# A fourth buffer for DMA-made weight sums, their loads asked for six steps ahead, and bias rows built in another ring

## The chip, the cores and the metric

The kernel runs on one core of one Trainium2 chip. The metric is the device time of one execution in microseconds (us), the median of several. One execution was profiled as well; all rows come from it.

## The reference, cut to what matters

One layer of an encoder over 512 tokens of width 1024, all in float32:

```python
x = x + 0.5 * swiglu(rmsnorm(x, ffn1_norm), w1, w3, w2)       # feed-forward "a", width 2816
h = rmsnorm(x, mix_norm)
x = x + hybrid_mixer(h, ...)      # h @ w_in, dilated attention (3 groups, T5 bias), grouped-query attention, gates, w_out
x = x + 0.5 * swiglu(rmsnorm(x, ffn2_norm), w1, w3, w2)       # feed-forward "b"
return rmsnorm(x, final_norm)

def swiglu(x, w1, w3, w2):
    return (silu(x @ w1) * (x @ w3)) @ w2
```

The dilated attention adds a bias `bias_tab[t5_bucket(rel)]` to its scores and masks keys outside a window.

## The kernel before, in words

**Three products for one.** A float32 matrix product is made of three products on TensorE: each operand is split into a rounded half H (cast on ScalarE, L211 for weights) and a remainder L (subtraction on VectorE, L212), and `mm3` (L226 to L228) adds H*H, H*L and L*H in PSUM.

**Weights.** All weights pass as tiles of 128x1024. A raw tile comes by DMA into a ring, L211 and L212 make its halves in the ring `wh`/`wl`, and TensorE uses them. Rings (`BUFS`, L19) have a fixed number of buffers: `wr` for plain tiles, and in three stages `wa`, `wt`, `ws` besides. A buffer is loaded again once the last instruction that reads its old tile is done.

**Strassen steps.** In the feed-forward stages (first products of `w1`, `w3`) and in the query/key part of the mixer (`project_qk`), two feature tiles f, f+1 by two halves of the contraction are multiplied by a scheme with seven products instead of eight. The seven steps of a pair are `A11, S1, S2, A12, S3, S4, A22`; each is 24 matmuls of 256 columns. Steps A11, A12 and A22 use a block of the weight as it is. S1 and S3 use a sum of two blocks, which DMA makes: SP loads one block into a `wt` tile (L192), then POOL issues a second transfer that adds the other block into it (L193). S2 and S4 use sums that VectorE makes in a `ws` tile: S2 = S1 + A11 and S4 = S2 + A12 (L210). So a `wt` tile of S1 is read by L210 as well as by L211 and L212. The pairs are interleaved, so that in the steady state the order is A11, S3 (of the pair before), S1, S4 (before), S2, A22 (before), A12. After each step an eviction (`evict`, L452) moves or adds the PSUM bank into a tile `c1` (128x1024, two buffers in pool `c`) or `c2`; after A22, L440 writes the gated result `gg` and `c1` is free. S3 and A22 use the same bank, so A22 can start only when the eviction of S3 (L466, in the query/key stage L726) is done.

**Groups.** Feed-forward "a" makes features 0 to 3 plainly, then three groups by Strassen steps (4 to 7, 8 to 15, 16 to 21), and after each group the rows of `w2` (`blocks`), eight rows d, each ended by an eviction that adds to `x`. "b" is the same with 0 and 1 plain. The query/key stage has one group of five pairs, with evictions of its own (L711).

**Bias rows.** During the `w2` rows of the first group of "a", `side` calls `bias_rows(g)` after rows d = 0, 1, 2: two small loads (a one-hot table and a mask), one product on TensorE (L594), one combination on VectorE (L595) and a store to DRAM from POOL's queue (L596). The three tiles `onehot`, `vmask` and `v` have one buffer each in a pool of their own.

**Order.** TensorE runs in the order in which the program is written. The instructions of the other engines and the DMA issues of SP, ACT and POOL are ordered by a planner at build time: from its own costs it takes, on each engine, the instruction that is ready by its reckoning, and the one that was written first when several are. On the chip each engine and each queue then goes strictly in that order, so one that waits holds up all behind it. When weights are asked for in the written order is set by `todo` (L117): tiles in the order of use, except that a `wt` tile is moved ahead by `EARLY` steps; `ring` (L148) says whether a buffer can be had.

**Row norms.** The sums of squares of a stage's input are made while it already runs; `stat_r` (L382) takes their row sums on TensorE, POOL computes the power -1/2 (L380), and `stat_R` (L391) spreads it by transposes on TensorE (L395). The evictions of the stage's first products wait for it.

Of the kernel before, what the change touches and what calls it, by code (L numbers as in the profile page):

```python
# [11 lines left out]
F32 = mybir.dt.float32  # L12
F32R = mybir.dt.float32r
AF = mybir.ActivationFunctionType
ALU = mybir.AluOpType
PSUM = bass.MemoryType.PSUM
DRAM = bass.MemoryType.DRAM

BUFS = {"wr": 3, "wa": 3, "ws": 2, "wt": 3, "wh": 3, "whx": 1}  # L19
EARLY = 4  # L20
GROUPS = {"a": (4, 8, 16, 22), "b": (2, 8, 16, 22)}
PAIRS = ((0, 0), (1, 0), (0, 1), (0, 2), (1, 1), (1, 2), (2, 0), (3, 0), (2, 1), (2, 2), (3, 1), (3, 2))
NSQ = 10
# [21 lines left out]
V0, V1, V2 = 383, 255, 255  # L45
# [24 lines left out]
class Layer:  # L70
    def __init__(self, ctx, tc, a):
        self.tc, self.nc, self.a = tc, tc.nc, a
        ctx.enter_context(tc.manual_schedule(engines={mybir.EngineType.PE}))
        pool = lambda n, **k: ctx.enter_context(tc.tile_pool(name=n, **k))
        self.dram = pool("dram", bufs=1, space=DRAM)
        self.cst = pool("cst", bufs=1)
        self.wb = pool("wb", bufs=1)
        self.tmp = pool("tmp", bufs=4)
        self.psm = pool("psm", bufs=4, space=PSUM)
        self.psa = pool("psa", bufs=4, space=PSUM)  # L80
        nc = self.nc
        c = self.cst
        self.x = [c.tile([128, T], F32, name=f"x{d}") for d in range(NK)]
        self.par = c.tile([128, 48], F32, name="par")
        nc.scalar.dma_start(self.par, a["par"])
        self.ident = c.tile([128, 128], F32, name="ident")
        self.ones = c.tile([128, 1], F32, name="ones")
        nc.vector.memset(self.ones, 1.0)
        self.mhalf = c.tile([128, 4], F32, name="mhalf")
        nc.vector.memset(self.mhalf, -0.5)  # L90
        nc.scalar.activation(self.ones, self.ones, AF.Copy)
        self.r = c.tile([128, 8], F32, name="r")
        self.R = c.tile([128, T], F32, name="R")
        nc.gpsimd.memset(self.R, 0.0)
        self.acc = c.tile([128, T], F32, name="acc")
        self.open_h()
        self.gate_d = self.dram.tile([16, 128, T], F32, name="gate_d")
        self.qk_d = self.dram.tile([2 * NSQ, 128, T], F32, name="qk_d")
        self.items = ([("v", 0), ("v", 1), ("sw", 0), ("v", 2)] + [("g", j) for j in range(2)]
                      + [("qk", f) for f in range(NSQ, 12)] + [("g", j) for j in range(2, 9)]  # L100
                      + [("b", g) for g in range(3)] + [("g", j) for j in range(9, 16)])
        span = {"v": ("wav", 4), "qk": ("waq", 2), "g": ("wg", 1), "b": ("wb", 4)}
        self.order = self.ffn_order("a")
        for kind, n in self.items:
            if kind == "sw":
                self.order += [("swq", at) for at in self.slots(range(0, NSQ, 2))]
                continue
            name, m = span[kind]
            self.order += [(name, m * n + i) for i in range(m)]
        self.order += [("wab", i) for i in range(12)] + [("wo", i) for i in range(8)]  # L110
        self.order += self.ffn_order("b")
        self.raws, self.tiles, self.used, self.wx, self.TQ = {}, [], 0, None, None
        self.cap = len(self.order)
        self.rings = {k: [] for k in BUFS}
        self.index = {it[:2]: n for n, it in enumerate(self.order)}
        self.kind = [self.home(it) for it in self.order]
        self.todo = sorted((n for n, t in enumerate(self.kind) if t != "ws"), key=lambda n: n - EARLY * (self.kind[n] == "wt"))  # L117

    @staticmethod
    def slots(fs):  # L120
# [27 lines left out]
    def ring(self, tag, n, done, last):  # L148
        held, bufs = self.rings[tag], BUFS[tag]
        pool = self.wb if tag in ("wr", "wh") else self.wx  # L150
        if pool is None or (len(held) >= bufs and held[-bufs] >= done):
            return None
        held.append(last)
        if tag[:2] != "wh":
            return pool.tile([128, 1024], F32, tag=tag, name=tag, bufs=bufs)
        return tuple(pool.tile([128, 1024], F32R, tag=t, name=t, bufs=bufs) for t in ("wh", "wl"))
# [427 lines left out]
    def bias_rows(self, g):  # L584
        nc = self.nc
        n = (V0, V1, V2)[g]
        o = (0, V0, V0 + V1)[g]
        t = {}
        for k, p in (("onehot", 32), ("vmask", 8), ("v", 8)):
            t[k] = self.bp.tile([p, V0], F32, tag=k, name=k)[:, :n]  # L590
            if k != "v":
                nc.sync.dma_start(t[k], self.a[k][:, o:o + n])
        ps = self.aux("bps")
        nc.tensor.matmul(ps[:8, :n], self.rel[:, 8 * g:8 * g + 8], t["onehot"], start=True, stop=True)  # L594
        nc.vector.scalar_tensor_tensor(t["v"], ps[:8, :n], 8.0, t["vmask"], op0=ALU.mult, op1=ALU.add)  # L595
        nc.gpsimd.dma_start(self.vd[:, o:o + n], t["v"])  # L596

    def bias_spread(self, h):
        src = self.vd[h]
# [620 lines left out]
```

## Time and profile before

| What | Value |
|---|---|
| Median of three runs | 1286.1 us (1284.0 to 1286.13) |
| The profiled execution's own time | 1290.42 us |
| Its span, first to last instruction | 1288.7 us |
| Mean granted TensorE clock | 0.996 of full |
| Bytes moved by DMA | 181.91 MB, mean 141 GB/s |
| wt loads: base (SP, L192) and added block (POOL, L193) | 48 of each, 512 KB |
| S2 sums on VectorE (L210, ws<-wt,wa) | 24 |

A row of the timeline has start, duration, engine, line, operation, output<-inputs, count, and in brackets the time that the engine was idle before it and what ended that. A row of a waits view has the total, the number of times and the longest. DMA issues are shown on their queue (SPq, POOL) by the time of issue, not of landing. "issue" means that the profile shows nothing that was waited for.

### The profile page before, as it was taken

Reading aid. Unit: us, or ns where it says so; the run is one execution under the profiler, and the core shown is the slowest. Engines: PE = TensorE matmul, PEld = TensorE weight load, DVE = VectorE, ACT = ScalarE, POOL = GpSimd, SP = SyncE. Lnnn points to the kernel's source line nnn. Section 1 sums busy time; section 2 is a strip of 40 time slices with the busy share of each in tenths; the row PEclk is TensorE's granted clock in tenths of the full one; section 3 lists DMA queues with packets and bytes.
Section 4 is the critical chain, followed back from the end, with each engine's and each line's share of the span. In section 5 each row is a group of like instructions: output and inputs, shape, how many; then the busy total and the mean of one; then the engine's idle time right before and its main releaser. Section 6 shows DMA issues by size and latency. Waiting matters only on the chain.

```text
span 1288.7 us, 19953 instructions
## 1 busy us (share of the span) xinstructions
PE 1270.0 (99%) x8002; PEld 1124.2 (87%) x8002; DVE 883.7 (69%) x1339; ACT 586.5 (46%) x867; POOL 119.2 (9%) x124
## 2 busy tenths in 40 slices
PE   9999999999999999999999999999999999999997
PEld 6897999899889999877888878888889889988996
DVE  7784688468784685767557898655577857774775
ACT  8551355145453443634334466543475415432553
POOL 1011110010210112100001100000201001000001
PEclk9999999999999999999999999999999999999998
DMA  8775677352474866533232310345537537643422
GB/s 301 193 181 171 174 194 183 98 131 67 131 196 131 198 179 219 175 116 92 83 111 82 115 49 25 127 159 190 179 99 179 164 98 185 171 152 99 99 82 66
DMA packets 85549, 181.91 MB, mean 141 GB/s; under 512 B 12480, under 2 KB 19024, under 8 KB 85456
## 3 DMA queue, kind: packets, MB, share of 16 engines
q1 hardware_dynamic: 67904, 140.74, 33.5%
q0 software_dynamic: 16832, 39.34, 15.2%
q8 instruction: 63, 1.03, 0.3%
q10 hardware_dynamic: 720, 0.55, 0.1%
q14 instruction: 30, 0.25, 0.1%
HBM read 168.98 MB, written 15.29 MB: 143 GB/s over the span
## 4 chain that ended last, share of the span: by engine, by line
PE 89%; DVE 4%; issue 2%; ACT 1%; DMA 1%; POOL 0%; SPq 0%; POOLq 0%; DVEq 0%; ACTq 0%
PE mm L226 23%; PE mm L228 23%; PE mm L227 23%; PE Y L226 3%; PE Y L228 3%; PE Y L227 3%; PE X L226 2%; PE X L228 2%; PE X L227 2%; DVE wl L212 1%; PE S L780 1%; PE mm L831 1%; PE Tb L970 1%; PE T L849 1%; PE Sb L227 0%
## 5 line engine op out<-in xcount | busy, mean ns | idle before, releaser
L211 ACT CAST wh<-wr 128x1024 fp32r<-128x1024 f32 x142 | 148.7, 1049 | 218.7 <-PE mm L227 137.6
L212 DVE TENSOR_TENSOR wl<-wr,wh 128x1024 fp32r<-128x1024 f32 x142 | 173.3, 1221 | 56.4 <-ACT wh L211 56.0
L226 PE MATMUL mm<-hH,wh 128*128 128x256 f32 (+1 forms) x600 | 200.0, 333 | 0.5 <-ACT hH L362 0.4
L228 PE MATMUL mm<-hH,wl 128*128 128x256 f32 (+1 forms) x600 | 196.5, 327 | 1.0 <-DVE wl L212 1.0
L227 PE MATMUL mm<-hL,wh 128*128 128x256 f32 (+1 forms) x600 | 196.0, 327 | 0.3 <-DVE hL L363 0.3
L226 PE MATMUL mm<-gg,wh 128*128 128x512 f32 (+1 forms) x376 | 143.2, 381 | 0.0
L228 PE MATMUL mm<-gg,wl 128*128 128x512 f32 (+1 forms) x376 | 142.6, 379 | 0.0
L227 PE MATMUL mm<-gg,wh 128*128 128x512 f32 (+1 forms) x376 | 142.5, 379 | 0.0
L226 PEld LDWEIGHTS mm<-hH,wh 128*128 128x128 f32 x600 | 112.7, 188 | 14.8 <-issue 3.2
L228 PEld LDWEIGHTS mm<-hH,wl 128*128 128x128 f32 x600 | 112.6, 188 | 12.3 <-DVE wl L212 1.4
L227 PEld LDWEIGHTS mm<-hL,wh 128*128 128x128 f32 x600 | 112.7, 188 | 10.4 <-DVE hL L363 0.9
L211 ACT CAST wh<-wa 128x1024 fp32r<-128x1024 f32 x48 | 50.4, 1050 | 102.5 <-PE mm L227 48.0
L494 DVE TENSOR_TENSOR u<-mm,R 128x512 f32<-128x512 f32 (+1 forms) x52 | 33.8, 649 | 85.2 <-PE mm L228 84.9
L226 PE MATMUL mm<-TH,wh 128*128 128x256 f32 x304 | 85.5, 281 | 2.7 <-DVE c L466 2.7
L228 PE MATMUL mm<-TH,wl 128*128 128x256 f32 x304 | 85.6, 281 | 0.0
L227 PE MATMUL mm<-TL,wh 128*128 128x256 f32 x304 | 85.4, 281 | 0.0
L226 PEld LDWEIGHTS mm<-gg,wh 128*128 128x128 f32 x376 | 71.0, 189 | 15.3 <-issue 1.1
L228 PEld LDWEIGHTS mm<-gg,wl 128*128 128x128 f32 x376 | 70.8, 188 | 14.2
L227 PEld LDWEIGHTS mm<-gg,wh 128*128 128x128 f32 x376 | 70.9, 189 | 13.8
L211 ACT CAST wh<-ws 128x1024 fp32r<-128x1024 f32 x48 | 50.4, 1051 | 69.3 <-PE mm L227 51.7
L212 DVE TENSOR_TENSOR wl<-wt,wh 128x1024 fp32r<-128x1024 f32 x48 | 58.6, 1222 | 34.0 <-ACT wh L211 33.6
L211 ACT CAST wh<-wt 128x1024 fp32r<-128x1024 f32 x48 | 50.3, 1050 | 65.0 <-PE mm L227 37.1
(233 smaller groups left out, 3181.5 us busy)
## 6 DMA issues: line engine op xcount, KB each, us to landing
wr<-in_w2a SPq DMA_DIRECT2D x22, 512.0 KB, 3.5
wr<-in_w2b SPq DMA_DIRECT2D x22, 512.0 KB, 3.5
wt<-in_w13b SPq DMA_DIRECT2D x20, 512.0 KB, 3.5
wa<-in_w13b SPq DMA_DIRECT2D x20, 512.0 KB, 4.5
wt<-in_w13b POOLq DMA_DIRECT2D x20, 512.0 KB, 5.8
wt<-in_w13a SPq DMA_DIRECT2D x18, 512.0 KB, 3.5
wt<-in_w13a POOLq DMA_DIRECT2D x18, 512.0 KB, 6.3
wa<-in_w13a SPq DMA_DIRECT2D x18, 512.0 KB, 4.4
```

Of the source, the lines that this page charges most:

```text
L211: self.nc.scalar.copy(H, raw)
L212: self.nc.vector.tensor_sub(L, raw, f32(H))
L226: mm(out, lH, rH, start=start, stop=False, skip_group_check=more)
L227: mm(out, lH, rL, start=False, stop=False, skip_group_check=more)
L228: mm(out, lL, rH, start=False, stop=stop, skip_group_check=more)
L494: nc.vector.tensor_mul(u, ps, R)
L780: nc.tensor.matmul(*args, start=True, stop=True)
L831: nc.tensor.matmul(oc, v, p, start=st, stop=sp)
L849: nc.tensor.transpose(ps[:, 128 * b:128 * b + 128], P[h][:, c0 + 128 * b:c0 + 128 * b + 128], self.ident)
L970: nc.tensor.transpose(pt[:, 128 * j:128 * j + 128], P[h, j][:, 128 * k:128 * k + 128], self.ident)
```

## The change

The ring `wt` gets a fourth buffer in all three stages that use it. `EARLY` becomes six steps in the feed-forward stages and stays at four for queries and keys. `bias_rows` no longer has three tiles of its own: it takes a tile of the eviction ring `c1`, uses 32 rows of its first half for the one-hot table and 8 rows of its second half for the mask, and the combination writes its result over the mask.

```diff
-BUFS = {"wr": 3, "wa": 3, "ws": 2, "wt": 3, "wh": 3, "whx": 1}
-EARLY = 4
+BUFS = {"wr": 3, "wa": 3, "ws": 2, "wt": 4, "wh": 3, "whx": 1}
+EARLY = {"a": 6, "b": 6, "q": 4}
...
-        self.todo = sorted((n for n, t in enumerate(self.kind) if t != "ws"), key=lambda n: n - EARLY * (self.kind[n] == "wt"))
+        self.todo = sorted((n for n, t in enumerate(self.kind) if t != "ws"), key=lambda n: n - (EARLY[self.order[n][0][2]] if self.kind[n] == "wt" else 0))
...
-        t = {}
-        for k, p in (("onehot", 32), ("vmask", 8), ("v", 8)):
-            t[k] = self.bp.tile([p, V0], F32, tag=k, name=k)[:, :n]
-            if k != "v":
-                nc.sync.dma_start(t[k], self.a[k][:, o:o + n])
+        both = self.cp.tile([128, 1024], F32, tag="c1", name="bias")
+        t = {"onehot": both[:32, :n], "vmask": both[:8, 512:512 + n]}
+        for k in t:
+            nc.sync.dma_start(t[k], self.a[k][:, o:o + n])
         ps = self.aux("bps")
         nc.tensor.matmul(ps[:8, :n], self.rel[:, 8 * g:8 * g + 8], t["onehot"], start=True, stop=True)
-        nc.vector.scalar_tensor_tensor(t["v"], ps[:8, :n], 8.0, t["vmask"], op0=ALU.mult, op1=ALU.add)
-        nc.gpsimd.dma_start(self.vd[:, o:o + n], t["v"])
+        nc.vector.scalar_tensor_tensor(t["vmask"], ps[:8, :n], 8.0, t["vmask"], op0=ALU.mult, op1=ALU.add)
+        nc.gpsimd.dma_start(self.vd[:, o:o + n], t["vmask"])
```

## The prediction

> **What bounds the kernel now.** I read the page first: the span, the engines' shares and the chain that ended last.
>
> ```profile
> span 1288.7 us, 19953 instructions
> PE 1270.0 (99%) x8002; PEld 1124.2 (87%) x8002; DVE 883.7 (69%) x1339; ACT 586.5 (46%) x867; POOL 119.2 (9%) x124
> PE 89%; DVE 4%; issue 2%; ACT 1%; DMA 1%; POOL 0%; SPq 0%; POOLq 0%; DVEq 0%; ACTq 0%
> ```
>
> TensorE is busy 99% of the span and is 89% of the chain. The change takes no matmul away, so all it can win is time in which TensorE waits or runs at a lowered clock. So the next view is what TensorE waited for (total, times, longest), and then the places of those waits in the timeline.
>
> ```profile
> PE mm L226 <- DVE c L466: 2.7, 2, 2.1
> ...
> PE bps L594 <- DMA onehot<-in_onehot: 0.3, 1, 0.3
> ...
> 468.30 0.36 PE L226 MATMUL mm<-TQH,wh 128*128 128x256 f32 x1 [0.67 <-DVE c L726]
> 469.34 0.39 PE L228 MATMUL mm<-TQH,wl 128*128 128x256 f32 x1 [0.57 <-DVE wl L212]
> 564.35 0.88 PE L831 MATMUL mm<-PT,V 128*64 128x128 f32 x12 [1.85 <-DVE PT L851]
> 1013.02 0.35 PE L226 MATMUL mm<-TH,wh 128*128 128x256 f32 x1 [0.60 <-DVE c L466]
> 1136.53 0.35 PE L226 MATMUL mm<-TH,wh 128*128 128x256 f32 x1 [2.07 <-DVE c L466]
> 564.30:567.80 3.50, 3.45 (x27) 2.85 (x28) 2.93 (x11) 0.27 (x1) 0.00 (x0) 1.00 0.47 150
> 1137.60:1141.00 3.40, 3.40 (x18) 3.40 (x18) 2.96 (x3) 2.04 (x3) 0.00 (x0) 0.50 0.88 352
> ```
>
> There is little to win. The waits on an eviction (L466, L726) or a weight half (L212) lie at the end of a group of Strassen steps: 0.67 and 0.57 us in the query/key stage, 0.60 and 2.07 us in the second feed-forward stage. Each time TensorE waits for VectorE. The last two rows are windows (busy time of each engine, then the granted clock, the DMA share and GB/s). After the 2.07 us wait the clock is 0.50 for 3.40 us; after the 1.85 us wait of the attention stage it stays 1.00.
>
> Why was VectorE late there? These are its own rows, with its idle time in brackets, and then its idle time before the sums of L210, by what ended it (total, times).
>
> ```profile
> 72.64 1.22 DVE L210 TENSOR_TENSOR ws<-wt,wa 128x1024 f32<-128x1024 f32 x1 [3.04 <-DMA wt<-in_w13a]
> 466.32 1.23 DVE L210 TENSOR_TENSOR ws<-wt,wa 128x1024 f32<-128x1024 f32 x1 [5.13 <-issue]
> 996.69 1.23 DVE L210 TENSOR_TENSOR ws<-wt,wa 128x1024 f32<-128x1024 f32 x1 [3.79 <-DMA wt<-in_w13b]
> 1098.71 1.23 DVE L210 TENSOR_TENSOR ws<-wt,wa 128x1024 f32<-128x1024 f32 x1 [3.22 <-DMA wt<-in_w13b]
> 1120.20 1.23 DVE L210 TENSOR_TENSOR ws<-wt,wa 128x1024 f32<-128x1024 f32 x1 [4.63 <-issue]
> ...
>   issue: 18.0, 4
>   DMA wt<-in_w13b: 13.9, 6
>   DMA wt<-in_w13a: 9.7, 4
>   DMA wt<-in_waq: 4.4, 1
>   DMA wa<-in_w13b: 1.0, 1
> ```
>
> VectorE stands still 46.0 us in 15 pieces (18.0 + 13.9 + 9.7 + 4.4) before the sum S2 = S1 + A11, because the tile wt of S1, which two transfers make, has not landed. There are 24 such sums (nine and ten in the feed-forward stages, five for queries and keys). One stands in VectorE's order right behind the last read of its ws buffer, steps before its own product is due, so what is queued behind it waits for no need of its own. TensorE pays only when the piece is long: 3.04 us at 72.64 costs nothing, 3.79 costs 0.60, 5.13 costs 0.67 + 0.57, and 4.63 with 3.22 of 21 us earlier not yet worked off costs 2.07. The cover is thus about 3.2 us (3.79 less 0.60).
>
> **The change part by part.**
>
> *A fourth wt buffer.* The loads, from the queues of SP and POOL (rows merge neighbours, x2 is two DMAs):
>
> ```profile
> 1088.16 2.33 SPq L192 DMA_DIRECT2D wt<-in_w13b  x2
> 1108.46 2.10 SPq L192 DMA_DIRECT2D wt<-in_w13b  x2
> ...
> 1114.49 1.20 POOL L193 DMA_DIRECT2D wt<-in_w13b  x1 [18.35 <-DVE ws L210]
> ```
>
> wt loads come in pairs, an S1 and an S3 of neighbouring pairs of feature tiles, each as the tile three back in its ring is read for the last time. So the S1 tile that the sum at 1120.20 needs could start only at 1108.46, the first of its pair. Its base transfer and the accumulating one (issued at 1114.49) are in at 1120.2, 11.7 us after the start. With four buffers each load takes the place of the one before it in the list: this one moves to the second place of the pair at 1088.16, about 1090.1 (1088.16 + 2.33 - 0.37 for the DMA itself), 18 us earlier. At 11.7 us a load both transfers are in by 1101.8, and the sum can be reached at 1115.6 (4.63 before 1120.20): 13.8 us to spare. The wait goes to zero, and so do those at 996.69, 1098.71 and 466.32, as the query/key stage shares the ring size. What is late next? The other operand, wa, keeps three buffers; it ended 1.0 us of the idle time. The steady traffic is the same: as many bytes, in the same places of the queues.
>
> Gain on the path: 2.07 + 0.60 + 0.67 + 0.57 = 3.9 us.
>
> *The lowered clock.* 3.40 us at 0.50 cost 1.7 us. If it belongs to the 2.07 us wait, it goes too. One of the two waits near 2 us was followed by it and one was not, so I do not count on it: bounds 0 and 1.7, and I take 0, as the timed runs' own 4.3 us below this execution say that some of its losses are not theirs.
>
> [...]
>
> *The first loads of a stage.* Four tiles instead of three are filled at once: one more base and one more accumulating transfer move into the stage's beginning.
>
> ```profile
> 24.07 1.04 SPq L192 DMA_DIRECT2D wt<-in_w13a  x2
> 25.64 1.94 POOL L380 TENSOR_TENSOR r<-ms,mhalf 128x4 f32<-128x4 f32 x1 [7.76 <-DVE ms L379]
> 28.75 0.60 PE L395 MATMUL rb<-ident,r 128*128 128x128 f32 x4
> 30.98 2.54 POOL L193 DMA_DIRECT2D wt<-in_w13a  x2 [3.40 <-DMA wt<-in_w13a]
> ...
> 20.00:30.00 10.00, 10.00 (x51) 8.35 (x51) 9.17 (x9) 7.20 (x9) 1.94 (x1) 1.00 1.01 334
> ```
>
> The DMA engines are full there (share 1.01), so 1 MB more at 334 GB/s makes the transfers behind it about 3.1 us later. TensorE is busy 10.00 of 10.00 us in that window, so there is cover now, of unknown size: bounds 0 and 3.1 us. I take 0, because S1's first load is out earlier and the next weights of ring wr are ahead of it in the order. The accumulating DMA also passes POOL's power (L380), on which the row norms wait; that is the last rival.
>
> *Six steps instead of four* only move the wt loads ahead in the order in which they are asked for, past two weight tiles of ring wr. No load can start before its buffer is free, and the starts above follow buffers. Two SP issues of wt take 1.04 us here, so a wr load behind them is that much later; bounds 0 and 1.0 us, no wr transfer is among TensorE's waits, and I take 0. The cover is the ring itself: wr is loaded three tiles ahead.
>
> *Bias rows in the evictions' ring.*
>
> ```profile
> 95.54 1.22 DVE L440 TENSOR_TENSOR gg<-c,gg 128x1024 fp32r<-128x1024 f32 x1
> 102.96 0.33 SPq L592 DMA_DIRECT2D onehot<-in_onehot  x1
> 103.81 0.58 POOL L596 DMA_DIRECT2D vd<-v  x1 [18.86 <-DVE v L595]
> 105.39 0.31 SPq L592 DMA_DIRECT2D onehot<-in_onehot  x1
> 111.06 0.59 PE L594 MATMUL bps<-onehot,rel_bias 32*8 32x255 f32 x2
> ```
>
> Instruction counts stay: six loads, three products, three combinations (now in place), three stores. Before, one onehot buffer made the second load wait for the first product (issue at 102.96), and TensorE waited 0.3 us for it. Now rows 0 and 1 take the two c1 buffers, free when the group's last L440 ends (96.8), so the load of row 1 is in before its product: gain 0.3 us. Row 2 waits for the store of row 0, issued on POOL at 103.81, and then its load; SP needed 2.4 us from one onehot load to the next in the old order (105.39 - 102.96), so two such legs from 103.8 end by 108.7 and the product at 111.06 still has 2.4 us of cover. What stands behind that SP wait are weight loads three tiles ahead. If the cover were gone, its excess would be TensorE's wait. The next eviction's c1 comes a row stage later: nothing.
>
> Sum: 3.9 + 0.3 = 4.2 us, against this execution's own 1290.4 us (span 1288.7 and 1.7 around it). The timed median is 1286.1 us, 4.3 below it. I take the gain over in full, since 15 of 24 sums wait and not a stray one: 1286.1 - 4.2 = 1281.9 us.
>
> **Rivals.**
>
> *The clock too.* If the lowered stretch is in the timed runs and is the wait's, 1281.9 - 1.7 = 1280.2 us. For it: the place of the row. Against it: the wait at 564.35 without one.
>
> *Nothing to measure.* The waits of TensorE are only the excess over a cover of about 3.2 us; transfers quicker by 1 to 2 us in the unprofiled runs would leave 0.3 to 1.5 us of them, and the change then has that to win: 1284.6 to 1285.8, middle 1285.2. The same comes out if the planner, which orders VectorE's work again for the new program, puts another early instruction in front of the late L466. For it: the 4.3 us by which the timed runs are shorter. Against it: the long waits of VectorE are in three stages.
>
> *Slower: POOL's power behind an accumulating DMA.* In the first feed-forward stage POOL computes r from 25.64 to 27.58, and TensorE needs it at 28.75: cover 1.2 us. With the fourth buffer and higher place in the order the wt bases may go out before 24.07, and an accumulating DMA be put ahead of the power; POOL then stands until the base has landed. In the order of now that was 30.98, and two of them end at 33.52: r at 35.5, TensorE waits 6.7 us, and less the 4.2 won that is 2.5 us slower; with a lowered clock after so long a wait (1.7) 4.2: 1290.3 us. It decides from the point where a base that lands after about 25.6 stands before the power on POOL. For it: POOL is idle 7.76 us before the power, and a planner likes to fill that. Against: now it puts the DMAs behind.
>
> **How the numbers follow.** About 0.2% (2.6 us) is what a measurement tells from no change: faster is below 1283.5, slower above 1288.7. The forecast (waits gone, clock as it was) 0.42, the clock too 0.22, nothing to measure 0.22, POOL's power or another start of a stage that costs more than the gain 0.14. So faster 0.64, same 0.22, slower 0.14. The low end is the fastest of the three runs, 1284.0, less the whole 5.9: 1278.1. The high end takes in the no-gain case with a start that costs 1 to 2 us: 1287.5; the slow case is left out. The forecast's own range, with TensorE's waits gone, is 1279.5 to 1283.5.
>
> **What would show it.** Right: VectorE's idle time before L210 falls from 46.0 us to under 10, TensorE's rows for L466, L726 and the 0.57 us of L212 and the onehot row are gone, the wt loads keep their places but reach one tile further, and no half clock in the last third. Wrong step by step: S2 sums still wait over 3 us for wt (the fourth buffer isn't used early); a new TensorE row for rb or L380 near 28 us (the slow rival); a wait of bps for onehot near 111 us (the bias ring); or the waits gone and the time unchanged (they were not in the timed runs). The prediction is wrong if a replanned order puts a new stall elsewhere that is of the size of those removed.

## The result, and the profile after

| Kernel | Median us (range) | Kernel before beside it | Ratio, 95% interval |
|---|---|---|---|
| changed | 1293.48 (1292.9 to 1293.85) | 1286.05 | 1.0061 (1.0048 to 1.0074) |

The change makes the kernel 0.6% slower, about 7.8 us. The forecast was 1281.9 us. The profiled execution took 1292.9 us (span 1291.1). From line 585 on, the changed kernel's line numbers are one lower (L831 is L830).

The first fence is the kernel after: the chain by engine, what TensorE waited for, and the idle time of VectorE before L210.

```profile
PE 92%; DVE 3%; DMA 2%; ACT 1%; issue 1%; SPq 0%; POOL 0%; POOLq 0%; DVEq 0%
...
PE mm L226 <- DVE t L445: 7.6, 1, 7.6
...
  DMA wa<-in_w13b: 5.5, 2
  DMA wa<-in_w13a: 2.6, 1
```

All that the prediction said would go did go: no wt is waited for any more (46.0 us of VectorE's idle time are gone, the rest is for wa), and no row of L466, L726 or onehot stands among TensorE's waits. In their place is one wait that was not there before, 7.6 us for the tile t that L445 makes: the first evictions of feed-forward a. The chain of the kernel after shows, in order of time, what it hangs on (start, us, what; rows of under 0.1 us are left out).

```profile
24.11 1.42 SPq L190
25.59 0.47 SPq L192
26.10 9.80 DMA wa<-in_w13a
36.00 1.23 DVE ws L210
37.23 1.14 DVE wl L212
38.36 0.61 DVE t L445
39.01 0.80 PE mm L226
```

A weight tile is in the chain: the wa tile asked for at 26.10, which lands 9.80 us later. The sum S4 of the first Strassen pair (L210, ws<-ws,wa) waits for it, then come its other readers, and only then the eviction that TensorE needs. That tile is the A12 block of features 4 and 5, whose own product is several steps away. L445 does not use it; it only stands behind it. So the next thing to read is the order. The same place in the kernel before (chosen rows of the timeline: start, duration, engine, line, operation):

```profile
19.60 0.48 SPq L190 DMA_DIRECT2D wa<-in_w13a  x1
29.44 0.59 ACT L397 COPY R<-rb 128x512 f32<-128x512 f32 x1 [1.61 <-PE rb L395]
34.48 1.05 ACT L211 CAST wh<-wa 128x1024 fp32r<-128x1024 f32 x1
30.06 1.29 DVE L445 TENSOR_TENSOR t<-mm,R 128x512 f32<-128x512 f32 x2
42.44 1.22 DVE L210 TENSOR_TENSOR ws<-ws,wa 128x1024 f32<-128x1024 f32 x1
```

and in the kernel after, again chosen rows:

```profile
19.50 0.48 SPq L192 DMA_DIRECT2D wt<-in_w13a  x1
25.82 1.21 POOL L193 DMA_DIRECT2D wt<-in_w13a  x1 [8.20 <-DMA wt<-in_w13a]
26.67 1.96 POOL L380 TENSOR_TENSOR r<-ms,mhalf 128x4 f32<-128x4 f32 x1
28.69 0.65 PE L395 MATMUL rb<-ident,r 128*128 128x128 f32 x4
31.06 1.21 DVE L210 TENSOR_TENSOR ws<-wt,wa 128x1024 f32<-128x1024 f32 x1
35.93 1.04 ACT L211 CAST wh<-wa 128x1024 fp32r<-128x1024 f32 x1 [4.84 <-DMA wa<-in_w13a]
36.88 0.58 ACT L397 COPY R<-rb 128x512 f32<-128x512 f32 x1
36.00 1.23 DVE L210 TENSOR_TENSOR ws<-ws,wa 128x1024 f32<-128x1024 f32 x1 [2.59 <-DMA wa<-in_w13a]
38.28 1.28 DVE L445 TENSOR_TENSOR t<-mm,R 128x512 f32<-128x512 f32 x2
```

Before, ScalarE copied R at 29.44, right behind the transposes, and cast the wa tile 5 us later; VectorE evicted at 30.06 and made the S4 sum 12 us later. After, both pairs stand the other way round. R's transposes are on time (28.69 against 28.75), but the copy of R stands behind a cast that waits 4.84 us for the wa tile (36.88), and L445 stands behind the S4 sum. On SP the first wt base (19.50) has taken the place of a wa load (19.60). The wait has a second price; columns are the window, its length, busy time of TensorE's matmuls, its weight loads, VectorE, ScalarE and POOL, then granted clock, DMA share, GB/s:

```profile
31.42:34.90 3.48, 0.00 (x0) 0.00 (x0) 1.99 (x2) 0.00 (x0) 1.24 (x1) 1.00 1.09 262
34.95:45.10 10.15, 6.09 (x14) 4.79 (x15) 7.28 (x9) 6.02 (x8) 1.20 (x1) 0.50 1.05 290
```

3.48 us after TensorE comes to a stand its clock is halved, and it stays so for 10.15 us, 6.09 of them with matmuls. Fourteen matmuls took 6.1 us there instead of 14 x 0.23 = 3.2 (at the clock of 1.00 before the wait they start 0.23 us apart): 2.9 us more. So 7.6 + 2.9 = 10.5 us lost, against about 4 won.

### The profile page after: what moved, and what is told of

It reads as the page before. It is cut to its first block, busy times and chain, and to the rows that moved or that the text cites. A ratio compares the mean times of both kernels' runs of the same rounds, so it can differ in the third digit from the quotient of the medians.

```text
span 1291.1 us, 19957 instructions
## 1 busy us (share of the span) xinstructions
PE 1270.1 (98%) x8002; PEld 1123.6 (87%) x8002; DVE 889.5 (69%) x1339; ACT 587.0 (45%) x867; POOL 118.5 (9%) x124
## 4 chain that ended last, share of the span: by engine, by line
PE 92%; DVE 3%; DMA 2%; ACT 1%; issue 1%; SPq 0%; POOL 0%; POOLq 0%; DVEq 0%
PE mm L226 24%; PE mm L227 23%; PE mm L228 23%; PE Y L226 3%; PE Y L227 3%; PE Y L228 3%; PE X L226 2%; PE X L228 2%; PE X L227 2%; PE S L779 1%; PE mm L830 1%; PE Tb L969 1%; PE T L848 1%; DMA wa<-in_w13a 1%; DVE wl L212 1%
## 5 line engine op out<-in xcount | busy, mean ns | idle before, releaser
L212 DVE TENSOR_TENSOR wl<-wr,wh 128x1024 fp32r<-128x1024 f32 x142 | 173.6, 1223 | 56.8 <-ACT wh L211 56.4
L227 PEld LDWEIGHTS mm<-hL,wh 128*128 128x128 f32 x600 | 113.4, 189 | 10.5 <-DVE hL L363 0.9
L212 DVE TENSOR_TENSOR wl<-wt,wh 128x1024 fp32r<-128x1024 f32 x48 | 58.7, 1223 | 38.1 <-ACT wh L211 37.6
L212 DVE TENSOR_TENSOR wl<-wa,wh 128x1024 fp32r<-128x1024 f32 x48 | 58.6, 1222 | 31.6 <-ACT wh L211 31.4
```

What stands on the lines that cost most here:

```text
L212: self.nc.vector.tensor_sub(L, raw, f32(H))
L227: mm(out, lH, rL, start=False, stop=False, skip_group_check=more)
```

## The experiments

Theory 1: asking for wt six steps early makes the planner put instructions of the A12 tile ahead of R's copy (ScalarE) and of the first evictions (VectorE), and the loss is this order. Theory 2: the transfers themselves, the fourth tile's above all, crowd the start. Theory 3: POOL's power behind an accumulating DMA, the slower rival of the prediction. The runs went to chips on which the kernel before took 1287.13 us (the first four) and 1287.7 us (the last four), so the ratios are what is compared.

**Four steps early again** (e1_early4)

```diff
-EARLY = {"a": 6, "b": 6, "q": 4}
+EARLY = {"a": 4, "b": 4, "q": 4}
```

> The changed kernel with the wt loads asked for four steps early in the feed-forward stages, as before; the fourth wt buffer and the bias rows in c1 stay. Theory 1 (order): asking six steps early makes the planner put the ScalarE cast and the VectorE sum of the second group's A12 tile ahead of the copy of R (L397) and of the first evictions (L445), and these wait for that tile's transfer; then here the copy of R stands first again, TensorE's 7.6 us wait for t (L445) at 31 us and the half clock behind it are gone, and with the S2 waits gone too the time is 1282 to 1283 us. Theory 2 (crowding): the fourth tile's first loads, 1 MB more, delay the transfers at the start of feed-forward a; then the wait stays and the time is about 1293 us. Theory 3 (POOL's power behind an accumulating DMA): the power (L380) stands first again if the order is the cause, 1282 to 1283 us.

Measured: 1283.11 us (1282.3 to 1283.7), ratio 0.996 (0.9948 to 0.9972). Its timeline at the start of a:

```profile
30.33 0.59 ACT L397 COPY R<-rb 128x512 f32<-128x512 f32 x1 [1.62 <-PE rb L395]
35.36 1.05 ACT L211 CAST wh<-wa 128x1024 fp32r<-128x1024 f32 x1
30.95 1.29 DVE L445 TENSOR_TENSOR t<-mm,R 128x512 f32<-128x512 f32 x2
...
  issue: 1.5, 1
  DMA wa<-in_w13b: 1.0, 1
```

R's copy comes before the cast, the evictions start as the copy ends, and TensorE has no wait there. The last two lines are all of VectorE's idle time before L210. Four wt buffers without the six steps win what was forecast. Theory 2 in its form "the fourth tile" falls.

**Three wt buffers, six steps early** (e2_ring3)

```diff
-BUFS = {"wr": 3, "wa": 3, "ws": 2, "wt": 4, "wh": 3, "whx": 1}
+BUFS = {"wr": 3, "wa": 3, "ws": 2, "wt": 3, "wh": 3, "whx": 1}
```

> The changed kernel with three wt buffers instead of four; six steps early and the bias rows in c1 stay. Theory 1 (order): the same order of R's copy and the cast arises without the fourth buffer, so TensorE's wait of about 7.6 us for t (L445) and the half clock stay, and the S2 sums wait for wt as before: 1286.1 + 7.6 + 3 to 1286.1 + 7.6 + 3 + 0.5 = about 1297 us. Theory 2 (crowding by the fourth tile): the start is as in the kernel before, about 1286 us. Theory 3 (POOL's power): two accumulating DMAs stand before the power here as well, about 1297 us.

Measured: 1296.83 us (1295.06 to 1298.94), ratio 1.0068 (1.0055 to 1.0082). TensorE's waits, and two lines of VectorE's idle time before L210:

```profile
PE mm L226 <- DVE t L445: 8.0, 1, 8.0
...
PE mm L226 <- DVE c L466: 0.7, 1, 0.7
...
PE mm L226 <- DVE c L725: 0.6, 1, 0.6
...
  DMA wt<-in_w13b: 11.4, 5
  DMA wt<-in_w13a: 11.4, 5
```

Both are there: the wait at the start without the fourth buffer, and the old waits for wt and on L466. The six steps alone make the loss. What the missing buffer adds to it is not resolved: by the ratios, 1.0068 against 1.0061, it is 0.9 us, less than their doubt.

**Bias rows in c1 alone** (e3_bias): `wt` 3 and four steps early as in the kernel before, `bias_rows` as in the change.

> The kernel before with the bias rows in c1 alone (three wt buffers, four steps early). All theories: no new wait at the start; TensorE's wait of 0.3 us for onehot goes, 1285.8 us, not to be told from 1286.1. If the c1 ring of the evictions delays something, it shows here as more than 1286.1.

Measured: 1286.73 us (1284.44 to 1289.7), ratio 0.9991 (0.9981 to 1.0001): no difference that can be measured. The wait for onehot is not among TensorE's waits; its 0.3 us can be neither confirmed nor excluded by the time.

**Two instructions held back** (e4_pin_both), the changed kernel with the S4 sum (n = 15) behind the second L445 and the cast of the A12 tile (n = 11) behind R's copy (the new lines only):

```diff
+            with self.tc.issue_after(self.ev[1].ins) if n == 15 else nullcontext(): self.nc.vector.tensor_add(raw, a, b)
+        with self.tc.issue_after(self.rcopy.ins) if n == 11 else nullcontext(): self.nc.scalar.copy(H, raw)
...
+        self.rcopy = nc.scalar.copy(self.R[:, s], pr[:, s])
+            self.ev = getattr(self, "ev", []) + [nc.vector.tensor_mul(t[1], ps, self.R)]
```

> The changed kernel (four wt buffers, six steps early) with two instructions held back by hand: the ScalarE cast of the second group's first A12 tile behind the copy of R (L397), and the VectorE sum S4 that uses that tile behind the first evictions (L445). The two accumulating DMAs stay before POOL's power, and the loads stay nearly as in the changed kernel. Theory 1 (order on ScalarE and VectorE): the 7.6 us wait and the half clock go, 1282 to 1284 us. Theory 2 (crowding by transfers): the wait stays, since the transfers are the same, about 1293 us. Theory 3 (POOL's power behind the accumulating DMA): the wait stays, about 1292 us.

Measured: 1287.19 us (1286.23 to 1289.4), ratio 0.9997 (0.9988 to 1.0005). Most of the loss is gone, but the 1282 to 1284 us expected by theory 1 were missed. The rows:

```profile
31.24 0.58 ACT L397 COPY R<-rb 128x512 f32<-128x512 f32 x1
31.35 1.22 DVE L210 TENSOR_TENSOR ws<-wt,wa 128x1024 f32<-128x1024 f32 x1
32.49 1.22 DVE L323 TENSOR_TENSOR TL<-T,TH 128x1024 fp32r<-128x1024 f32 x1
33.63 1.28 DVE L445 TENSOR_TENSOR t<-mm,R 128x512 f32<-128x512 f32 x2
34.37 0.80 PE L226 MATMUL mm<-hH,wh 128*128 128x512 f32 x1 [2.70 <-DVE t L445]
33.65:40.45 6.80, 6.08 (x14) 4.79 (x15) 3.31 (x6) 3.82 (x5) 2.10 (x2) 0.50 1.08 328
```

R is there at 31.82, and L445 starts at 33.63: the S2 sum and an L323, which wait for nothing, still stand before it. TensorE waits 2.7 us, and a half clock of 6.80 us begins before the wait is over, again with 14 slow matmuls. Whether that is all that is left, the next run had to show.

**The whole order put back** (e5_order_back): as above, and the S2 sum (n = 10), L322 and L323 held back too (cut to the lines that matter):

```diff
-            with self.tc.issue_after(self.ev[1].ins) if n == 15 else nullcontext(): ...
+            with self.tc.issue_after(self.ev[1].ins) if n in (10, 15) else nullcontext(): ...
...
+            with self.tc.issue_after(self.rcopy.ins) if c else nullcontext(): nc.scalar.copy(H, src)
+            with self.tc.issue_after(self.ev[1].ins) if c else nullcontext(): nc.vector.tensor_sub(L, src, f32(H))
```

> The changed kernel (four wt buffers, six steps early) with the order around the first evictions of feed-forward a put back by hand: on ScalarE the later casts L322 and the cast of the A12 tile stand behind the copy of R (L397), on VectorE the later L323 and the sums S2 and S4 of the first Strassen pair stand behind the first two evictions (L445). POOL's order and nearly all of SP's stay those of the changed kernel. Theory 1 (the order on ScalarE and VectorE is the whole loss): no wait of TensorE near 31 us, no half clock, 1283 us as with four steps early. In the run with two instructions held back 2.7 us of wait were left; under this theory they are the two VectorE instructions (S2 sum and L323, 1.22 us each) that still stood before L445. Theory 2 (the loads of six steps early are themselves late or in the way): a wait of 2 us or more stays at the start, or new waits for w tiles come, 1285 us or more.

Measured: 1284.38 us (1282.96 to 1284.61), ratio 0.9969 (0.9956 to 0.9981).

```profile
26.53 1.21 POOL L193 DMA_DIRECT2D wt<-in_w13a  x1 [8.29 <-DMA wt<-in_w13a]
27.39 1.63 POOL L380 TENSOR_TENSOR r<-ms,mhalf 128x4 f32<-128x4 f32 x1
29.81 0.59 ACT L397 COPY R<-rb 128x512 f32<-128x512 f32 x1 [3.78 <-PE rb L395]
30.43 1.29 DVE L445 TENSOR_TENSOR t<-mm,R 128x512 f32<-128x512 f32 x2
```

With the loads of six steps early, and POOL's power still behind the accumulating DMA, the wait and the half clock are gone. The transfers are hardly quicker: from 31.42 to 34.90 us the DMA engines move 265 GB/s here and 262 in the changed kernel, from 34.95 to 45.10 us 294 and 290. The time cannot be told from that of four steps. What the transfers of six steps cost by themselves is below what these ratios resolve. This settles it for theory 1.

**Only ScalarE's cast held back** (e6_pin_act): the second line of the first diff above, alone.

> The changed kernel with only the ScalarE cast of the A12 tile held back behind the copy of R; VectorE keeps its order, in which the S4 sum of that tile stands before the first evictions. If ScalarE alone holds the evictions, TensorE's 7.6 us wait falls to about 2.7 us and the time to about 1287 us. If VectorE holds them as well, the S4 sum still waits for the A12 transfer until about 36 us, L445 starts about 37.1 instead of 38.3 us, and the wait falls by only the 1.2 us of L212: about 1292 us.

Measured: 1292.62 us (1292.12 to 1292.87), ratio 1.0036 (1.0023 to 1.0048).

```profile
PE mm L226 <- DVE t L445: 5.8, 1, 5.8
PE rb L395 <- POOL r L380: 2.0, 2, 1.0
...
26.66 1.21 POOL L193 DMA_DIRECT2D wt<-in_w13a  x1 [8.36 <-DMA wt<-in_w13a]
36.35 1.23 DVE L210 TENSOR_TENSOR ws<-ws,wa 128x1024 f32<-128x1024 f32 x1 [2.79 <-DMA wa<-in_w13a]
37.50 1.28 DVE L445 TENSOR_TENSOR t<-mm,R 128x512 f32<-128x512 f32 x2
```

VectorE holds the evictions as well: with R copied early L445 starts at 37.50 us, behind the S4 sum, 0.8 us earlier than in the changed kernel. VectorE's order alone is enough to keep TensorE waiting, so undoing ScalarE's changes little. That ScalarE's alone would be enough too is read from the changed kernel's rows, where R is copied only by 37.46; no run put VectorE's order back and left ScalarE's. By the trace it is 0.8 us of the wait and 12 instead of 14 slow matmuls, 0.4 us; by the ratios 0.0025, 3.2 us. The intervals, 0.0013 to either side of each ratio, leave some 2.4 us of doubt on their difference, so the two agree, but no better than that.

The wait of L445 reads 5.8 and not 6.8 us because TensorE stood 1.0 us for r before it (the other of the two rb waits is at the end of the kernel, and the changed kernel has it too). That is theory 3's mechanism, at a seventh of the price that the prediction gave it, and not in every profile: the accumulating DMA before the power is issued at 26.66 here and at 25.82 in the changed kernel's profile, where the transposes were on time.

**Matmuls in the gap** (e7_fill), the changed kernel with

```diff
-            hooks = {12: squares, 23: self.stat_r, 28: self.stat_R, "T": (16, 2)}
+            hooks = {12: squares, 23: self.stat_r, 28: self.stat_R, 31: lambda ps=self.aux("fill"): [nc.tensor.matmul(ps, self.hH[0][:, :128], self.hH[0], start=True, stop=True) for _ in range(30)], "T": (16, 2)}
```

> The changed kernel with 30 matmuls of 512 columns (7.0 us at 232 ns) that compute nothing of use put into TensorE's order at the place where it waits 7.6 us, into a PSUM bank of their own. The wait's own length stays. If the half clock from 35 to 45 us comes from TensorE being idle, the granted clock stays at 1.00, the next 6 us of matmuls run at 232 instead of 427 ns, and the time falls by 6.06 x (1 - 232/427) = 2.8 us, to 1290.7 us. If it has another cause, the time stays at 1293.5 us.

Measured: 1292.48 us (1291.78 to 1293.63), ratio 1.0036 (1.0023 to 1.0049). Two windows, and an eviction that is as late as ever:

```profile
38.08 1.28 DVE L445 TENSOR_TENSOR t<-mm,R 128x512 f32<-128x512 f32 x2
31.00:39.00 8.00, 8.00 (x36) 6.58 (x36) 5.67 (x7) 3.16 (x5) 1.24 (x1) 1.00 1.08 292
39.00:45.00 6.00, 6.00 (x28) 4.92 (x27) 4.15 (x7) 3.30 (x6) 1.20 (x1) 1.00 1.00 273
```

The clock stays at 1.00 through the gap and behind it, where the changed kernel has 0.50 from 34.95 to 45.10: the half clock came from TensorE standing still. By the ratios it is worth 3.2 us, with 2.8 expected, and with the same doubt of some 2.4 us. The profiled execution itself (span 1291.3 us) is not shorter than that of the changed kernel. It waits 1.0 us for r, as the run before does, and 2.15 instead of 1.1 us at one place of the attention stage, with a half clock behind it:

```profile
570.55 1.13 PE L830 MATMUL mm<-PT,V 128*64 128x128 f32 x16 [2.15 <-DVE PT L850]
571.55:574.90 3.35, 3.35 (x10) 2.61 (x9) 1.84 (x6) 0.00 (x0) 0.00 (x0) 0.50 0.32 117
```

**Four steps in a, six in b** (e8_a4b6)

```diff
-EARLY = {"a": 6, "b": 6, "q": 4}
+EARLY = {"a": 4, "b": 6, "q": 4}
```

> Four wt buffers and the bias rows in c1, four steps early in feed-forward a and for queries and keys, six in feed-forward b. Theory 1: six steps early do nothing of their own, and only the order at the start of a made the loss; the time is that of four steps everywhere, 1283.1 us, within 1 us. If six steps early bring something in b, it is below that; if they cost something there (VectorE waited 5.5 us for wa in b), above 1284 us.

Measured: 1282.72 us (1282.47 to 1282.96), ratio 0.9958 (0.9945 to 0.9972). The same as four steps everywhere within the intervals. In b VectorE waits longer for wa,

```profile
  DMA wa<-in_w13b: 5.6, 2
```

and TensorE pays nothing for it. Both this kernel and the one with four steps everywhere are faster than the kernel before and than the changed one.

## Why the prediction was wrong, point by point

**Fourth wt buffer, 3.9 us: right.** VectorE's waits for wt are gone in every run with four buffers and are there in both with three. With the bias rows the forecast was 4.2 us; four steps early measured 1287.13 - 1283.11 = 4.0 us, by the ratio 0.4% (0.28 to 0.52%), 3.6 to 6.7 us. That it agrees to 0.2 us is in part chance: the four waits that were added up are those of one execution, and in the profile of e3_bias, also with three buffers, the same kind of wait comes to 1.3 + 0.6 + 0.5 = 2.4 us (on L725, L212 and L466). The forecast kernel exists, then: it is this one, and not the one that was changed.

**The lowered clock, counted at 0: its cause is the wait, its share open.** Matmuls in the gap kept the clock up (1.00 from 31 to 45 us in e7_fill, 0.50 from 34.95 to 45.10 in the changed kernel), so in feed-forward a the half clock came from the wait. In the four profiles whose longest wait of TensorE is 1.3 to 1.8 us (e1_early4, e3_bias, e5_order_back, e8_a4b6) the clock is 1.00 from 31 to 45 us and from 50 us to the last 15. That the 1.7 us of the kernel before were the price of its 2.07 us wait is inferred from this; no run filled that wait. And neither profile with three buffers besides (e2_ring3, e3_bias) has a wait that long on L466: it is 0.7 and 0.5 us there, without a half clock. How often the timed executions had it is not known.

**First loads of a stage, counted at 0: right.** Four buffers with four steps early have no wait at the start that the kernel before does not have.

**"Six steps instead of four ... bounds 0 and 1.0 us ... I take 0": this is the step that failed.** It asked only what the earlier loads do to the loads behind them. Between e1_early4 and the changed kernel only this number differs. It is worth 1.0061 - 0.996 = 0.0101 by the ratios, 13 us with a doubt of some 2.4; 1293.48 - 1283.11 = 10.4 us by the medians on two chips; and 9.2 us by the spans (1291.1 - 1281.9). The trace accounts for 10.5 us, the 7.6 us wait and the 2.9 us behind it; whether there is more is open. The loads are at most a small part of it: with the order put back they cost 0.9969 - 0.996 = 0.0009, 1.2 us, less than the doubt. The planner, given another order of loads, ordered ScalarE and VectorE anew as well, and in strictly ordered queues two instructions of a tile that lands at 35.9 came before two that TensorE waits for at 31. The prediction knew that the planner might put an early instruction in front of a late one. But it counted this only as a way to lose the gain again; its last line names a new stall by a replanned order as what would prove it wrong, without a place, a price or a look at the order of ScalarE and VectorE at the start of a. Why the planner reckons the A12 tile ready before R when the wt loads are two steps further ahead was not looked into; shown is only that this setting turns the order.

**The slower rival: the right place, another mechanism.** Its chance of 0.14 stood for "POOL's power or another start of a stage that costs more than the gain". The accumulating DMA did go ahead of the power, as feared. But its base was in by 25.8, not 31, so the power came 1.0 us later (26.67 against 25.64) and the transposes on time. In e5_order_back the same order on POOL costs nothing that can be seen, in e6_pin_act 1.0 us of TensorE. That the rival's 6.7 us wait was near the size of the real one (7.6) is chance, as its cause was another; its half clock (1.7) was too small: the real one cost 2.9.

**Bias rows, 0.3 us: the wait is gone, the time is too small to tell.**

## What to carry over

Where a planner orders the queues, a change in when one thing is asked for can move instructions that have nothing to do with it; so the order of every engine around the tightest waits of TensorE is part of the cost of such a change, in this case above all at the start of feed-forward a, where the row norm is due and the load of the wa tile took 9.8 us (the median of the 18 loads of wa from in_w13a is 3.3 us). An instruction that waits for a transfer costs what stands behind it in its queue, not what it feeds: here the cast that waited 4.84 us held back the copy of R until 36.88 us. When an edit has two parts, time them apart: here one part was worth some minus 4 us and the other 10 or more, and the sum showed neither.

## What the runs showed of the hardware

The half clocks behind the waits quoted here last 10.15 us in the changed kernel, 10.20 in e2_ring3 (34.75 to 44.95), 6.80 in e4_pin_both, 3.35 in the attention stage of e7_fill, and in e6_pin_act 6.75:

```profile
36.75:43.50 6.75, 5.26 (x12) 4.18 (x13) 6.70 (x9) 4.99 (x7) 1.20 (x1) 0.50 1.03 266
```

In the kernel before it is 3.40 us. So it was 3.40 and 3.35 us behind waits of 2.07 and 2.15, 6.80 and 6.75 behind 2.7 and 5.8, and 10.15 and 10.20 behind 7.6 and 8.0 us: the longer ones are near two and three times the shortest. The 1.85 us wait in the attention stage of the kernel before was not followed by a half clock: the clock is 1.00 from 564.30 to 567.80. So the three waits of 2.07, 2.15 and 2.7 us cost their own length and 1.7, 1.7 and 2.9 us more (half of 3.40 and of 3.35 us, and 6.08 us less 14 x 0.23): 14 slow matmuls behind 2.7 us, as many as behind 7.6. In e4_pin_both the clock fell at 33.65, 2.0 us after TensorE had stopped (34.37 - 2.70 = 31.67) and before it went on. These waits lie where TensorE is otherwise busy throughout: 21.46 of 23.50 us from 1113.0 to 1136.5 in the kernel before, where it waits 2.07, and 7.85 of 10.00 us from 568 to 578 in e7_fill, where it waits 2.15. It is not at the end of the kernel before: from 1280 to 1283 us it is busy for 0.99 us and waits 1.0 us for r, and the mean clock there is 0.66.
